# A hybrid encoder layer: convolution turned by halves of its channels, projections dealt out anew, and sums of the up projection in PSUM

## The chip, the cores and the metric

The kernel runs on one core of a Trainium2 chip. The metric is the device time of one execution in microseconds (us); a comparison takes the median of several runs. PE is TensorE, DVE is VectorE, ACT is ScalarE, POOL is GpSimd, SP is SyncE, which here only issues DMAs.

## The reference

One layer works on x (2048 tokens x 1024), in float32.

```python
proj = x @ w_in                       # 1024 -> 3*512 (Hyena) + 3*512 (attention) + 512 (memory queries)
y_h = hyena_mixer(hy_u, ...)          # short convolution, then twice: z = x_i * fft_long_conv(z)
y_d = diff_attention(rope(dq), rope(dk), dv, ...)   # 4 heads, two halves of 64
y_m = memory_attention(mq, mem, w_kv)               # 256 memory tokens
x = layer_norm(ALPHA * x + concat(y_h, y_d, y_m) @ w_out)
h = dwconv3(x @ w_up) ; g, u = split(h)             # 2 x 2816 columns
x = layer_norm(ALPHA * x + (silu(g) * u) @ w_down)
```

`fft_long_conv` multiplies the spectrum of the input, zero-padded to 4096 points, with that of a filter, which a small network makes from the positions.

## The kernel before

Matrix products of full precision are made of three passes: each operand is split into a high part and a low part, and `mm3` (line 146) adds high x high, high x low and low x high in PSUM. The split of a weight chunk is an ACT cast and a subtraction on POOL or DVE (`low`, line 144).

The kernel runs as five stages in a row: `project` (line 679), `diff_attention`, `out_proj`, `ffn_up` (line 1214) and `ffn_down`.

`project` has two weaves (`weave`, line 661). Each has a main generator and a fill generator. Every yield of the main work earns a credit of 6144 x R x its weight (1.0 if it names none), and the fill is stepped until the credit is used up, in columns that pass through PE. In the first weave `spectra` makes the filter spectra and the fill is the Hyena projections (`proj_u`); R is R1. In the second `conv` makes the two long convolutions and the fill is the memory projections, the queries, keys and values (`proj_qk` with the rotary embedding, `proj_v`), and the memory attention; R is R2. What is left of the fill when the main work ends runs alone. A scheduler then orders the instructions of each engine by a simulation of its own, so the order on an engine follows that of issue only roughly; `keep_in_program_order` pins single instructions. `after(cols, f)` (line 539) issues f when that many more columns have been issued to PE.

The FFT of 2048 points as 128 x 16 works on S, a tile of [128, 32, 256]: 32 rows of 256 channels. There are four runs (two orders x two halves of the 512 channels). In each, `first` multiplies 8 loads of [128, 2 rows, 256 channels] with the matrices `st` (lines 248, 249); the four DVE transposes of `turn` (line 253, 64 channels each) turn S in 32x32 blocks; `middle` takes 16 pairs of rows through a block product (line 273), the product with the filter's spectrum on DVE (lines 393 to 400), and a second block product back into S (line 405); `turn` again; `last` multiplies with `sb` (line 419), gates with the loaded `hu` on DVE (line 421) and stores to `zd` or `yh`. `middle` needs all channels of its rows, so all four transposes; `first` and `last` of one row need only their own channels. `pipeline` (line 232) staggers the steps of such a part. The `last` of a run and the `first` of the next share one pipeline.

`hu` (the three Hyena inputs after their short convolution) is written to DRAM by `turn_u` (line 570) in the first weave.

`ffn_up` multiplies by Winograd's form of Strassen's scheme: a unit (128 columns of gate and up over 1024 tokens) is seven products, each of 12 matmuls of 512 columns, b11, t2, t1, t3, b21, b22, t4, with operands made beforehand (`weight`, line 1239: DVE and POOL make the sums `s`, ACT and POOL split them, up to nine products ahead). Each product has a PSUM tile of its own out of six, and its result is combined with the partial sums p1, u2, u3, u4 on DVE (line 1290) into the two rows that the width-3 convolution reads (ACT line 1317, DVE scalar_tensor_tensor line 1319). There are 44 units, 22 for each half of the tokens.

Of the kernel before, what the change touches and what calls it, by code (L numbers as in the profile page):

```python
# [10 lines left out]
F32 = mybir.dt.float32  # L11
# [10 lines left out]
HW = 512  # L22
# [107 lines left out]
class Trunk:  # L130
# [15 lines left out]
    def mm3(self, out, sh, sl, mh, ml, start, stop):  # L146

        mm = self.nc.tensor.matmul
        mm(out, sh, mh, start=start, stop=False)  # L149
        mm(out, sh, ml, start=False, stop=False)  # L150
        mm(out, sl, mh, start=False, stop=stop)  # L151
# [99 lines left out]
    NT, WTB, WTT, WTC = 4, 1.0, 0.8, 1.95  # L251

    def turn(self, S):

        for c in range(0, CH, 64):
            v = S[:, :, c:c + 64].rearrange("p t c -> p c t")
            t = self.nc.vector.transpose(v, v)
            if c == 128:
# [82 lines left out]
    def load_u(self, t, i, u, hs):  # L341
        for k in range(2):
            self.dma(t[:, k], self.hu[i][:, 2 * u + k, :, hs])

# [8 lines left out]
    def conv(self, yp, sp, ph):  # L353
# [5 lines left out]

        def first(o, h):  # L360
            hs = slice(CH * h, CH * h + CH)

            def a0(u):
                xa[u] = self.hy(sp, "kr")
                if o:
                    self.dma(xa[u], self.zd[h][:, 2 * u:2 * u + 2])
                else:
                    self.load_u(xa[u], 0, u, hs)

            def a1(u):  # L370
                p = xa.pop(u)
                self.stage1(S, ph, u, p, p)

            return a0, a1
# [34 lines left out]
        def last(o, h):  # L409
            hs = slice(CH * h, CH * h + CH)  # L410

            def c0(u):
                xb[u] = self.hy(sp, "kr")
                self.load_u(xb[u], 1 + o, u, hs)

            def c1(u):
                ps = self.hy(ph, "h")
                for par in range(2):
                    nc.tensor.matmul(ps, self.sb[:, par], S[:, 16 * par + 2 * u:16 * par + 2 * u + 2], start=(par == 0), stop=(par == 1))
                z = self.hy(sp, "t")  # L420
                nc.vector.tensor_tensor(z, ps, xb.pop(u), ALU.mult)
                dst = self.zd[h] if o == 0 else self.yh.rearrange("(t1 t2) c -> t1 t2 c", t2=16)[:, :, hs]
                self.dma(dst[:, 2 * u:2 * u + 2], z)

            return c0, c1
# [4 lines left out]
        def both(*fs):  # L430
            def f(u):
                for g in fs:
                    g(u)
            return f

        yield from self.pipeline(8, first(*runs[0]))
        for i, run in enumerate(runs):
            yield from self.turn(S)
            yield from self.pipeline(16, middle(*run), self.WTB)
            yield from self.turn(S)  # L440
            c0, c1 = last(*run)
            if i + 1 < len(runs):
                a0, a1 = first(*runs[i + 1])
                yield from self.pipeline(8, [c0, a0, c1, a1], self.WTC)
            else:
                yield from self.pipeline(8, [c0, skip, c1])
# [100 lines left out]
    def proj_u(self, st, pp, quarter, ahead):  # L547
        nc = self.nc
        for cc in range(12):
# [11 lines left out]
            nat = lambda v: v.rearrange("p (t1 t2) -> p t1 t2", t2=16)  # L561
            nc.vector.tensor_scalar(t, h[:, 1:513], cw[:, 1, cc:cc + 1], self.cb[:, cc:cc + 1], ALU.mult, ALU.add)
            nc.vector.scalar_tensor_tensor(t, h[:, 0:512], cw[:, 0, cc:cc + 1], t, ALU.mult, ALU.add)
            nc.vector.scalar_tensor_tensor(tp.rearrange("p b (r t1) -> p t1 (b r)", r=4), nat(h[:, 2:514]),
# [3 lines left out]
    LATE = 17000  # L568

    def turn_u(self, st, pt, quarter, cc, tp):  # L570
# [6 lines left out]
        dst = self.hu[cc // 4][quarter].rearrange("(b r) t1 c -> (r t1) b c", r=4)  # L577
        nc.scalar.dma_start(dst[:, :, 128 * (cc % 4):128 * (cc % 4) + 128], ev)

    def proj_qk(self, pp, t0, rope, cc):  # L580
# [14 lines left out]
        nc.vector.tensor_tensor(q, q, rope[:, 0], ALU.mult)  # L595
        nc.gpsimd.tensor_tensor(rot, rot, rope[:, 1], ALU.mult)
        nc.vector.tensor_tensor(q, q, rot, ALU.add)
        out = self.s2.tile([128, 2, 512], F32R, name="qo", tag="hl", bufs=self.HL)
        nc.scalar.copy(out[:, 0], q)
        self.low(nc.vector, out[:, 1], q, out[:, 0])  # L600
        self.dma(self.qk[cc // 4][cc % 4][:, :, t0:t0 + 512], out)
# [72 lines left out]
    NB1, WIDE, HL = {}, 4, 2  # L674
    NB2 = dict(c_m2=4, c_ma=6, kr=6, ki=4, t=4)
    R1 = 0.605
    R2 = 0.521
# [536 lines left out]
    def ffn_up(self):  # L1214
# [5 lines left out]
        with ExitStack() as ctx:  # L1220
# [51 lines left out]
            def product(n, ps, name):  # L1272
                wh, wl = ops.pop(n)
                xh, xl = self.xo[name]
                for k in range(4):
                    self.mm3(ps, wh[:, k], wl[:, k], xh[:, k], xl[:, k], k == 0, k == 3)
                    next(fill, None)

            def unit(u):
                s, c = divmod(u, NF)  # L1280
                rows = [hp.tile([128, 1027], F32, name=f"row{g}", tag=f"row{g}") for g in range(2)]
                for g in range(2):
                    if s == 0:
                        nc.gpsimd.memset(rows[g][:, 1:2], 0.0)
                    else:
# [3 lines left out]
                p1, u2, u3, u4 = (sp.tile([128, 512], F32, name=t, tag="u", bufs=5) for t in ("p1", "u2", "u3", "u4"))  # L1289
# [8 lines left out]
                for j, (name, f) in enumerate(steps):  # L1298
                    weight(7 * u + j + self.AHEAD)
                    ps = pp.tile([128, 512], F32, name="pu", tag="u")  # L1300
                    product(7 * u + j, ps, name)
                    f(ps)
                    if j == 2:
                        p5 = ps
                    elif j == 3:
                        add(out[1][1], p5, u3)
                    elif j == 5 and stores:
# [201 lines left out]
```

## Time and profile before

| what | us |
|---|---|
| median of 3 runs | 3761.63 (3761.15 to 3763.39) |
| the profiled execution | 3758.56 |
| its span, first to last instruction | 3756.8 |
| PE busy | 3503.8 (93%) |
| DVE busy | 2548.0 (68%) |
| ACT busy | 1537.9 (41%) |
| POOL busy | 1711.6 (46%) |

The mean granted clock of TensorE is 0.965 of full speed. Matmuls overlap, so the duration of one (0.39 us) is more than the distance from one to the next. Times in the rows are counted from the first instruction. A row of waits names who waited, for whom, the total in us, how often, and the longest. A row of windows gives the stretch, its length, the busy time of each engine with the number of instructions in brackets, the granted clock, the busy share of the DMA engines and GB/s. A row of the timeline gives start, duration, engine, line, operation, tiles and shapes, the count of merged instructions, and in brackets the idle time before and what ended it.

### The profile page before, as it was taken

The numbers are of one execution on the slowest core, as the hardware profiler recorded it, in microseconds if no ns is written. First come the engines' busy times: TensorE is split into PE (matmuls) and PEld (weight loads), VectorE is DVE, ScalarE is ACT, GpSimd is POOL, SyncE is SP. The second block draws the span as 40 slices with busy tenths as digits, with TensorE's granted clock in tenths as the row PEclk, the third lists the DMA queues.
The fourth block names the chain that finished last, engine by engine and source line by source line (L and its number), as shares of the span: only waits on it lengthen the run. The fifth ranks groups of instructions, "written<-read, shape, count | busy, mean of one in ns | idle before, by whom it ended". The sixth has DMA issues, their size and how long they took to land.

```text
span 3756.8 us, 48083 instructions
## 1 busy us (share of the span) xinstructions
PE 3503.8 (93%) x16952; PEld 2843.6 (76%) x16952; DVE 2548.0 (68%) x2952; ACT 1537.9 (41%) x2903; POOL 1711.6 (46%) x1484
## 2 busy tenths in 40 slices
PE   8899988888888879999999998999989999899998
PEld 7788877565757667877877886887767888688887
DVE  7667647575857649888985444777877888622565
ACT  4443443333323337787884101433344443421211
POOL 3222313222222336666664223888866888610333
PEclk9999999999999989999999998999999999999999
DMA  6655568576757571213213445322233223443553
GB/s 161 194 176 164 181 194 216 168 209 191 205 170 193 155 170 44 75 41 86 58 42 104 138 151 174 87 79 83 75 116 96 80 82 84 168 141 113 175 180 132
DMA packets 536069, 502.43 MB, mean 134 GB/s; under 512 B 78216, under 2 KB 416780, under 8 KB 534292
## 3 DMA queue, kind: packets, MB, share of 16 engines
q1 hardware_dynamic: 273236, 343.08, 31.0%
q10 hardware_dynamic: 262592, 156.27, 14.4%
q8 instruction: 135, 2.21, 0.2%
q14 instruction: 106, 0.87, 0.1%
HBM read 369.20 MB, written 121.63 MB: 131 GB/s over the span
## 4 chain that ended last, share of the span: by engine, by line
PE 49%; POOL 5%; DMA 3%; DVE 2%; ACT 2%; issue 1%; ACTq 0%; SPq 0%; POOLq 0%; DVEq 0%
PE ps L149 7%; PE ps L151 7%; PE ps L150 7%; PE pu L149 5%; PE pu L150 5%; PE pu L151 5%; PE po L860 5%; POOL al L144 3%; PE pt L852 3%; PE ps L820 2%; PE ps L821 2%; DMA xr<-in_w_out_dram 1%; DVE t L1319 1%; POOL t L1322 1%; ACT t L1317 1%
## 5 line engine op out<-in xcount | busy, mean ns | idle before, releaser
L144 POOL TENSOR_TENSOR wl<-wr,wh 128x512 fp32r<-128x512 f32 x180 | 243.4, 1354 | 699.6 <-ACT wh L504 421.1
L149 PE MATMUL pu<-slot,ah 128*128 128x512 f32 x1232 | 491.2, 399 | 9.5 <-ACT slot L1056 5.6
L150 PE MATMUL pu<-slot,ah 128*128 128x512 f32 x1232 | 488.1, 396 | 0.0
L151 PE MATMUL pu<-slot,al 128*128 128x512 f32 x1232 | 486.4, 395 | 0.0
L149 PE MATMUL pp<-xh,wh 128*128 128x512 f32 (+2 forms) x1344 | 475.1, 354 | 10.0 <-ACT wh L504 3.7
L151 PE MATMUL pp<-xh,wl 128*128 128x512 f32 (+2 forms) x1344 | 457.3, 341 | 5.2 <-POOL wl L144 3.8
L150 PE MATMUL pp<-xl,wh 128*128 128x512 f32 (+2 forms) x1344 | 454.2, 338 | 0.9 <-DVE xl L144 0.9
L823 DVE TENSOR_REDUCE st<-ps 128x1 f32<-128x1024 f32 x256 | 312.1, 1220 | 55.1 <-PE ps L821 53.7
L1319 DVE SCALAR_TENSOR_TENSOR t<-row,fcw,t 128x1023 f32<-128x1023 f32 (+1 forms) x176 | 286.3, 1646 | 91.5 <-ACT t L1317 90.0
L144 POOL TENSOR_TENSOR al<-s,ah 128x512 fp32r<-128x512 f32 x176 | 294.7, 1676 | 35.5 <-ACT ah L1266 29.8
L827 ACT ACTIVATE e<-ps,st 128x1024 f32<-128x1024 f32 x256 | 287.1, 1124 | 35.1 <-DVE st L823 33.1
L149 PEld LDWEIGHTS pp<-xh,wh 128*128 128x128 f32 x1344 | 258.5, 192 | 48.5 <-issue 18.4
L151 PEld LDWEIGHTS pp<-xh,wl 128*128 128x128 f32 x1344 | 258.2, 192 | 41.9 <-issue 12.5
L150 PEld LDWEIGHTS pp<-xl,wh 128*128 128x128 f32 x1344 | 259.1, 193 | 35.4 <-issue 14.2
L149 PEld LDWEIGHTS pu<-slot,ah 128*128 128x128 f32 x1232 | 232.7, 189 | 69.9 <-DVE u L1290 8.5
L820 PE MATMUL ps<-kk,q 128*128 128x512 f32 x512 | 253.7, 495 | 26.2 <-DMA kk<-qk 15.1
L151 PEld LDWEIGHTS pu<-slot,al 128*128 128x128 f32 x1232 | 232.5, 189 | 55.5
L150 PEld LDWEIGHTS pu<-slot,ah 128*128 128x128 f32 x1232 | 233.4, 189 | 53.3
L151 PE MATMUL ps<-slot,gl 128*128 128x512 f32 x689 | 270.9, 393 | 0.0
L150 PE MATMUL ps<-slot,gh 128*128 128x512 f32 x689 | 270.7, 394 | 0.0
L149 PE MATMUL ps<-slot,gh 128*128 128x512 f32 x689 | 270.6, 393 | 0.0
L860 PE MATMUL po<-at,v 128*128 128x256 f32 x1024 | 269.3, 387 | 0.8
(228 smaller groups left out, 7869.6 us busy)
## 6 DMA issues: line engine op xcount, KB each, us to landing
wr<-in_w_in_dram ACTq DMA_DIRECT2D x224, 256.0 KB
slot<-in_ffn_w_up_dram ACTq DMA_DIRECT2D x88, 512.0 KB
gr<-gd SPq DMA_DIRECT2D x63, 448.0 KB
gd<-t SPq DMA_DIRECT2D x66, 256.0 KB
xr<-in_x_dram SPq DMA_DIRECT2D x64, 256.0 KB
dec<-in_c_dec_dram SPq DMA_DIRECT2D x32, 512.0 KB
c_m<-in_c_m_dram SPq DMA_DIRECT2D x128, 128.0 KB
kd<-ev ACTq DMA_DIRECT2D x64, 256.0 KB
```

The lines of the kernel that those rows point to most:

```text
L144: eng.tensor_tensor(lo, src, hi.bitcast(F32), ALU.subtract)
L149: mm(out, sh, mh, start=start, stop=False)
L150: mm(out, sh, ml, start=False, stop=False)
L151: mm(out, sl, mh, start=False, stop=stop)
L820: self.tc.keep_in_program_order(nc.tensor.matmul(o, qh, kk[c][:, ks], start=True, stop=False))
L821: self.tc.keep_in_program_order(nc.tensor.matmul(o, ql, kk[c][:, ks], start=False, stop=True))
L823: nc.vector.tensor_reduce(m, ps, AX.X, ALU.max, negate=True)
L827: nc.scalar.activation(e[:, 1024 * t:1024 * t + 1024], ps, AF.Exp, bias=m, accum_out=col(6 + 2 * t))
L852: self.tc.keep_in_program_order(nc.tensor.transpose(ps[:, j], e[:, 512 * g + 128 * j:512 * g + 128 * j + 128], self.ident))
L860: self.tc.keep_in_program_order(nc.tensor.matmul(P["ps"], P["v"][:, kb], P["at"][kb // 4][:, kb % 4], start=(kb == 0), stop=(kb == 15)))
L1317: nc.scalar.activation(v, rows[g][:, c0:c1], AF.Identity, bias=cb[:, cc:cc + 1], scale=cw[:, 1, cc:cc + 1])
L1319: nc.vector.scalar_tensor_tensor(v, rows[g][:, c0 + k - 1:c1 + k - 1], cw[:, k, cc:cc + 1], v, ALU.mult, ALU.add)
```

## The change

- `S` is worked in the outer stages by halves of its channels: `first` and `last` take [128, 4 rows, 128 channels] at a time, the four steps of one half before those of the other. Two of the four transposes (`turn_half`) remain at each boundary; the other two are issued inside the outer pipelines (`turns`).
- DRAM tiles `hu` and `zd` are laid out by quarters of the channels, and `turn_u` writes in that layout.
- The weights of the yields and the ratios R1 and R2 are new, so the fill is dealt out otherwise.
- The rotary arithmetic is issued 6500 columns after the projection, its split and store after 10500. Its tiles have 8 buffers in place of 4.
- In `ffn_up` a unit has three PSUM tiles, pa, pb and pc. b11 and then b21 are added in pa, t2, t3 and t4 in pb, t1 and b22 in pc; between them DVE or ACT reads the sums so far. `u4` is gone, and the first row's first half is an ACT copy.

```diff
-    def mm3(self, out, sh, sl, mh, ml, start, stop):
+    def mm3(self, out, sh, sl, mh, ml, start, stop, more=False):
...
-        self.hu = [t(f"hu{k}", [4, 16, 32, HW]) for k in range(3)]
-        self.zd = [t(f"zd{h}", [128, 16, CH]) for h in range(2)]
+        self.hu = [[t(f"hu{k}{p}", [128, 16, 128]) for p in range(4)] for k in range(3)]
+        self.zd = [t(f"zd{p}", [128, 16, 128]) for p in range(4)]
...
-    NT, WTB, WTT, WTC = 4, 1.0, 0.8, 1.95
+    NT, WTT, WTB, WTC, WTH = 4, 1.63, 0.92, 1.08, 1.0
+
+    def turn_part(self, S, i):
+
+        v = S[:, :, 64 * i:64 * i + 64].rearrange("p t c -> p c t")
+        return self.nc.vector.transpose(v, v)
...
+    def turn_half(self, S, p):
+        for i in range(2):
+            t = self.turn_part(S, 2 * p + i)
+            if i == 0:
+                self.tc.keep_in_program_order(t)
+            yield self.WTH
+        for _ in range(2):
+            yield self.WTH
...
+        def rows(par, v):
+
+            p, u = v // 4, v % 4
+            return S[:, 16 * par + 4 * u:16 * par + 4 * u + 4, 128 * p:128 * p + 128]
+
         def first(o, h):
...
+            def a0(v):
+                p, r = part(v)
+                xa[v] = quarter(self.hy(sp, "kr"))
+                self.dma(xa[v], (self.zd if o else self.hu[0])[2 * h + p][:, r])
+
+            def a1(v):
+                x = xa.pop(v)
+                for par in range(2):
+                    ps = quarter(self.hy(ph, "h"))
+                    nc.tensor.matmul(ps, self.st[:, par], x, start=True, stop=True)
+                    nc.scalar.copy(rows(par, v), ps)
...
-        yield from self.pipeline(8, first(*runs[0]))
+        def turns(plan):
+
+            def f(v):
+                for i in plan.get(v, ()):
+                    self.tc.keep_in_program_order(self.turn_part(S, i))
+            return f
+
+        a0, a1 = first(*runs[0])
+        yield from self.pipeline(8, [a0, skip, skip, a1, turns({3: (0,), 5: (1,)})], self.WTC)
         for i, run in enumerate(runs):
-            yield from self.turn(S)
+            yield from self.turn_half(S, 1)
             yield from self.pipeline(16, middle(*run), self.WTB)
-            yield from self.turn(S)
+            yield from self.turn_half(S, 0)
             c0, c1 = last(*run)
+            c0 = both(turns({0: (2,), 2: (3,)}), c0)
             if i + 1 < len(runs):
                 a0, a1 = first(*runs[i + 1])
-                yield from self.pipeline(8, [c0, a0, c1, a1], self.WTC)
+                yield from self.pipeline(8, [c0, a0, c1, a1, turns({3: (0,), 5: (1,)})], self.WTC)
             else:
-                yield from self.pipeline(8, [c0, skip, c1])
+                yield from self.pipeline(8, [c0, skip, c1], self.WTC)
...
     LATE = 17000
+    ROT = (6500, 10500)
...
+        def turned():
+            nc.vector.tensor_tensor(q, q, rope[:, 0], ALU.mult)
+            nc.gpsimd.tensor_tensor(rot, rot, rope[:, 1], ALU.mult)
+            nc.vector.tensor_tensor(q, q, rot, ALU.add)
...
+        self.after(self.ROT[0], turned)
+        self.after(self.ROT[1], parted)
...
-    NB1, WIDE, HL = {}, 4, 2
+    NB1, WIDE, HL = {}, 8, 2
...
-    R1 = 0.605
-    R2 = 0.521
+    R1 = 0.52
+    R2 = 0.81
...
-                steps = (("b11", lambda p: nc.scalar.copy(p1, p)),
-                         ("t2", lambda p: add(u2, p, p1)),
-                         ("t1", lambda p: add(u4, p, u2)),
-                         ("t3", lambda p: add(u3, p, u2)),
-                         ("b21", lambda p: add(out[0][0], p, p1)),
-                         ("b22", lambda p: add(out[0][1], p, u4)),
-                         ("t4", lambda p: add(out[1][0], p, u3)))
+                pa, pb, pc = (pp.tile([128, 512], F32, name=t, tag="u") for t in ("pa", "pb", "pc"))
+
+                def after_t3():
+                    add(u3, pb, p1)
+                    add(out[1][1], pc, u3)
+
+                steps = (("b11", pa, lambda: nc.scalar.copy(p1, pa)),
+                         ("t2", pb, lambda: add(u2, pb, p1)),
+                         ("t1", pc, None),
+                         ("t3", pb, after_t3),
+                         ("b21", pa, lambda: nc.scalar.copy(out[0][0], pa)),
+                         ("b22", pc, lambda: add(out[0][1], pc, u2)),
+                         ("t4", pb, lambda: add(out[1][0], pb, p1)))
```

`last` changes as `first` does: one load of `hu` per step, and `rows(par, v)` as the moving operand. `quarter` views a tile of [128, 2, 256] as [128, 4, 128], and `part(v)` gives the half and the four rows of step v.

## Rows read from the trace of the kernel before

**Rows 1.** Windows of stages: length, PE, PEld, DVE, ACT, POOL busy, clock, DMA.

```profile
0.00:527.00 527.00, 484.92 (x3296) 434.11 (x3297) 360.01 (x376) 220.12 (x429) 149.86 (x113) 0.95 0.59 178
...
527.00:1290.00 763.00, 650.74 (x2806) 490.09 (x2805) 498.03 (x617) 256.17 (x548) 191.85 (x167) 0.93 0.67 189
1290.00:1373.00 83.00, 80.99 (x406) 66.83 (x405) 31.94 (x52) 37.09 (x84) 40.17 (x34) 1.00 0.62 164
...
2342.00:3246.00 904.00, 884.42 (x3816) 710.81 (x3815) 728.32 (x642) 362.27 (x523) 719.53 (x574) 0.99 0.30 86
```

**Rows 2.** Waits of PE, first row of 0 to 527, the others of 527 to 1290.

```profile
PE h L273 <- DVE S L257: 25.7, 4, 9.1
...
PE h L419 <- DVE S L257: 33.8, 4, 11.2
PE h L273 <- DVE S L257: 20.2, 3, 10.9
...
PE h L248 <- DMA kr<-hu: 4.4, 4, 1.8
```

**Rows 3.** Windows of turns plus 12 us: the first stage's four, the convolution's eight.

```profile
sum 116.60, PE 90.41 PEld 84.61 DVE 101.78 ACT 36.23 POOL 21.61; mean PE 22.60 PEld 21.15 DVE 25.45 ACT 9.06 POOL 5.40
...
573.70:603.50 29.80, 19.84 (x95) 16.25 (x96) 29.24 (x29) 9.60 (x23) 7.71 (x6) 0.84 0.91 216
...
1246.80:1275.80 29.00, 21.94 (x74) 13.51 (x73) 23.86 (x19) 6.41 (x17) 6.17 (x8) 0.82 0.39 120
sum 232.50, PE 162.94 PEld 116.32 DVE 203.97 ACT 63.77 POOL 55.47; mean PE 20.37 PEld 14.54 DVE 25.50 ACT 7.97 POOL 6.93
```

**Rows 4.** Timeline of one turn of the convolution, 690 to 760.

```profile
697.24 17.08 DVE L257 STREAM_TRANSPOSE S<-S 128x2048 f32<-128x2048 f32 x4
...
707.03 0.39 PE L151 MATMUL pp<-xh,wl 128*128 128x512 f32 x1
...
714.38 3.78 PE L419 MATMUL h<-S,sb 128*128 128x512 f32 x4 [6.96 <-DVE S L257]
```

**Rows 5.** Windows between turns, sums: four middle stretches, then four outer ones.

```profile
sum 353.00, PE 327.82 PEld 273.36 DVE 246.77 ACT 131.09 POOL 104.39; mean PE 81.95 PEld 68.34 DVE 61.69 ACT 32.77 POOL 26.10
...
sum 130.80, PE 121.87 PEld 72.68 DVE 39.46 ACT 43.00 POOL 24.35; mean PE 30.47 PEld 18.17 DVE 9.86 ACT 10.75 POOL 6.09
```

**Rows 6.** Waits of DVE in the convolution, 527 to 1290.

```profile
DVE q L595 <- DMA rot<-q: 65.0, 15, 9.2
```

**Rows 7.** Windows of the up projection: ten units, ten units, twenty units.

```profile
2832.00:3222.00 390.00, 390.00 (x1681) 315.61 (x1680) 331.26 (x276) 155.30 (x219) 317.98 (x256) 1.00 0.27 75
2364.00:2559.00 195.00, 195.00 (x842) 157.85 (x840) 155.52 (x136) 77.99 (x110) 161.53 (x127) 1.00 0.28 79
2559.00:2760.00 201.00, 197.77 (x841) 156.91 (x839) 158.25 (x140) 76.39 (x110) 165.07 (x131) 1.00 0.28 79
```

**Rows 8.** Timeline of one unit of the up projection: PE, DVE and ACT.

```profile
2605.30 0.40 PE L151 MATMUL pu<-slot,al 128*128 128x512 f32 x1
...
2609.95 5.16 DVE L1319 SCALAR_TENSOR_TENSOR t<-row,fcw,t 128x1023 f32<-128x1023 f32 x3
2615.03 0.68 DVE L1290 TENSOR_TENSOR u<-pu,p 128x512 f32<-128x512 f32 x1
2616.29 2.88 DVE L1250 TENSOR_TENSOR s<-slot 128x512 f32<-128x512 f32 x1 [0.59 <-POOL s L1250]
...
2620.36 1.76 DVE L1250 TENSOR_TENSOR s<-s,slot 128x512 f32<-128x512 f32 x1 [0.58 <-POOL al L144]
...
2622.76 0.69 DVE L1290 TENSOR_TENSOR row<-pu,u 128x512 f32<-128x512 f32 x1
...
2627.00 1.24 ACT L1317 ACTIVATE t<-row,fcb,fcw 128x1023 f32<-128x1023 f32 x1
...
2628.28 1.28 DVE L1319 SCALAR_TENSOR_TENSOR t<-row,fcw,t 128x1023 f32<-128x1023 f32 x1 [3.03 <-ACT t L1317]
```

**Rows 9.** Waits of PE from the end of the up projection on, 3246 to 3757.

```profile
PE ps L149 <- DVE row L1290: 13.8, 1, 13.8
```

More of the change, by code (lines that the diff above doesn't have):

```diff
@@ L144, in low @@
         eng.tensor_tensor(lo, src, hi.bitcast(F32), ALU.subtract)
-    def mm3(self, out, sh, sl, mh, ml, start, stop):
+    def mm3(self, out, sh, sl, mh, ml, start, stop, more=False):
         mm = self.nc.tensor.matmul
-        mm(out, sh, mh, start=start, stop=False)
-        mm(out, sh, ml, start=False, stop=False)
-        mm(out, sl, mh, start=False, stop=stop)
+        mm(out, sh, mh, start=start, stop=False, skip_group_check=more)
+        mm(out, sh, ml, start=False, stop=False, skip_group_check=more)
+        mm(out, sl, mh, start=False, stop=stop, skip_group_check=more)
     def scratch(self, ctx):
@@ L249, in stage1 @@
             nc.scalar.copy(S[:, 16 * par + 2 * u:16 * par + 2 * u + 2], ps)
-    NT, WTB, WTT, WTC = 4, 1.0, 0.8, 1.95
+    NT, WTT, WTB, WTC, WTH = 4, 1.63, 0.92, 1.08, 1.0
+    def turn_part(self, S, i):
+        v = S[:, :, 64 * i:64 * i + 64].rearrange("p t c -> p c t")
+        return self.nc.vector.transpose(v, v)
     def turn(self, S):
[L255 to L258, printed above, removed]
+        for i in range(4):
+            t = self.turn_part(S, i)
+            if i == 2:
                 self.tc.keep_in_program_order(t)
@@ L339, in filters @@
                 yield from self.pipeline(16, [g0, skip, g1])
-    def load_u(self, t, i, u, hs):
-        for k in range(2):
-            self.dma(t[:, k], self.hu[i][:, 2 * u + k, :, hs])
     ENG = ["pppv"]
@@ L409, in last, with c0, c1 @@
         def last(o, h):
[L410 to L417, printed above, removed]
-                for par in range(2):
[L419 to L423, printed above, removed]
+            def c0(v):
+                p, r = part(v)
+                xb[v] = quarter(self.hy(sp, "kr"))
+                self.dma(xb[v], self.hu[1 + o][2 * h + p][:, r])
+            def c1(v):
+                p, r = part(v)
+                ps = quarter(self.hy(ph, "h"))
+                for par in range(2):
+                    nc.tensor.matmul(ps, self.sb[:, par], rows(par, v), start=(par == 0), stop=(par == 1))
+                z = quarter(self.hy(sp, "t"))
+                nc.vector.tensor_tensor(z, ps, xb.pop(v), ALU.mult)
+                q = 2 * h + p
+                dst = self.zd[q] if o == 0 else self.yh.rearrange("(t1 t2) c -> t1 t2 c", t2=16)[:, :, 128 * q:128 * q + 128]
+                self.dma(dst[:, r], z)
             return c0, c1
@@ L594, in proj_qk, with parted @@
             self.dma(rot[32 * b:32 * b + 32], q[s:s + 32])
[L595 to L601, printed above, removed]
+        def turned():
+            nc.vector.tensor_tensor(q, q, rope[:, 0], ALU.mult)
+            nc.gpsimd.tensor_tensor(rot, rot, rope[:, 1], ALU.mult)
+            nc.vector.tensor_tensor(q, q, rot, ALU.add)
+        def parted():
+            out = self.s2.tile([128, 2, 512], F32R, name="qo", tag="hl", bufs=self.HL)
+            nc.scalar.copy(out[:, 0], q)
+            self.low(nc.vector, out[:, 1], q, out[:, 0])
+            self.dma(self.qk[cc // 4][cc % 4][:, :, t0:t0 + 512], out)
+        self.after(self.ROT[0], turned)
+        self.after(self.ROT[1], parted)
         yield
@@ L1270, in weight, with product @@
                     self.up_raw(u + 2)
-            def product(n, ps, name):
+            def product(n, ps, name, first):
                 wh, wl = ops.pop(n)
@@ L1275, in product @@
                 for k in range(4):
-                    self.mm3(ps, wh[:, k], wl[:, k], xh[:, k], xl[:, k], k == 0, k == 3)
+                    self.mm3(ps, wh[:, k], wl[:, k], xh[:, k], xl[:, k], first and k == 0, k == 3, not first)
                     next(fill, None)
@@ L1288, in unit @@
                 out = [[rows[g][:, 2 + 512 * t:514 + 512 * t] for t in range(2)] for g in range(2)]
[L1289 removed]
+                p1, u2, u3 = (sp.tile([128, 512], F32, name=t, tag="u", bufs=5) for t in ("p1", "u2", "u3"))
                 add = lambda o, x, y: nc.vector.tensor_tensor(o, x, y, ALU.add)
[L1291 to L1307 removed]
+                pa, pb, pc = (pp.tile([128, 512], F32, name=t, tag="u") for t in ("pa", "pb", "pc"))
[9 more added lines that the diff above has]
+                         ("t4", pb, lambda: add(out[1][0], pb, p1)))
+                for j, (name, ps, f) in enumerate(steps):
+                    weight(7 * u + j + self.AHEAD)
+                    product(7 * u + j, ps, name, j < 3)
+                    if f:
+                        f()
+                    if j == 5 and stores:
                         store(*stores.pop())
```

24 lines of the change are left out of this document (8 added, 16 removed).

## The prediction

> **What bounds the kernel now.** I read the stages' windows first, then who waited for whom in each. TensorE (PE) is busy in every stage and ends the kernel, so time can come only from its idle stretches, from its slower clock, or from new waits put into its order. [rows 1] gives the idle time. The first stage (filter spectra as main work, the Hyena projections woven in as fill) is 527 us long with 42 idle. The convolution, up to its last output at 1290, is 763 us with 112 idle at a mean clock of 0.93. The 83 us after it hold projections alone, with 2 idle. The up projection is 904 us with 20 idle. Since the last two are nearly full, the convolution is the place to look, and [rows 2] names its cause: PE waits for the DVE transposes of S, 54 us directly in the convolution and 26 in the first stage. Everything else in that list is small (the loads of `hu` cost 4.4 us).
>
> [rows 3] widens the view to each turn (four transposes) plus 12 us, since the clock falls after an idle spell. In the convolution eight such stretches lose 232.5 - 162.9 = 69.6 us of PE. Their granted clock is 0.84 in the first and 0.82 in the last, so 9.5 to 10.4 us of each 29 run at the lower of the two levels, where a matmul takes twice as long. If all idle time (8.7 us a turn) lies inside, the clock costs under 1 us a turn; if none does, 5. I take 2.6, so 21 for eight: a turn's price is 91 us in all. The first stage's four turns lose 116.6 - 90.4 = 26.2 us idle, and 8 more for the clock in the same proportion: 34 us.
>
> [rows 4] shows one turn. DVE holds 17.1 us of transposes; PE works on projections for 9.8 us after their start, runs out of them, and stands 7 us until S is turned.
>
> **The unit of fill.** One unit is 6144 columns, 12 matmuls of 512. In [rows 7] ten units of `ffn_up`, 84 such matmuls each, take 195.0 us, so one is 0.232 us and a fill unit 2.79. A yield of the main work earns weight x R units.
>
> **Change 1, the first stage.** A turn there earned 8 x 0.8 x 0.605 = 3.9 units, 10.8 us against 17 of transposes. It now earns 8 x 1.63 x 0.52 = 6.8 units, 18.9 us: the transposes are covered. The other 33 yields of a run earn 33 x (0.605 - 0.52) = 2.8 units, 7.8 us, less. This was taken from stretches that are nearly full (42 - 26 = 16 us idle in the rest of the stage, its start included), with main work still there to do. The total stays the same (162 yields' worth at 0.605, 188 at 0.52: 98 units each), so no fill is left over. Bounds: -34 if nothing else opens, -12 if thinner fill exposes other waits. I take **-28**.
>
> **Change 2, half turns.** Before, a turn in the convolution earned 8 x 0.8 x 0.521 = 3.3 units, 9.3 us, against 17.1. Now two of the four transposes stand at a boundary (8.5 us) with 4 x 1.0 x 0.81 = 3.2 units, 9.0 us, beside them. The other two are issued inside the outer pipelines, after the steps that fill their half of the channels and before the steps that read it. Nothing is removed: 32 transposes, the same matmuls, the same columns. Sixteen transposes only move to where DVE has room: in the four outer stretches of [rows 5] it is busy 39.5 of 130.8 us. There a transpose of 4.3 us can stand ahead of the product `z` (line 421), which frees a PSUM tile that PE needs two steps later. Bound: nothing, to 16 x 4.3 = 69 us if PE always waited it out. A step holds some 3 us of convolution and as much fill, so I stay near nothing: I leave 20 of the 91 us, for all of this together.
>
> **Change 3, projections spread.** By the weights the convolution earned 121 units and now earns 151, against some 155 wanted in all. The tail of pure projections goes into the stage. This gains nothing by itself, as the tail was full; it is the cover that change 2 uses. If the cover ran out before the convolution did, its last pipeline would stand bare.
>
> **Change 4, rotary later.** `q*rope` overwrites what the DMA `rot<-q` still reads, so it stands at the head of DVE's queue until that lands: 65.0 us in 15 waits [rows 6]. Behind it stand the products of `middle`, the turns and the weights' low parts. POOL's `rot*rope` waits likewise, with the low parts `wl` behind it. Issued 6500 columns (3 us of fill, more with convolution between) later, most of it is gone. The four rotary DMAs keep their place on SP's queue; the store of `qo` moves some 10500 columns back, so loads queued behind it on SP are held up less. PE's own idle time in the four middles is 353.0 - 327.8 = 25 us [rows 5]; I credit 9 of it. Changes 2 to 4 come to 91 - 20 + 9 = **-80**; bounds -115 (turns and most of the middle's idle gone) and -40.
>
> **Costed at nothing.** Loads of `hu` fall from two to one per step, with longer pieces; `yh` is stored in shorter ones. They are issued two or three steps ahead behind the fill, and uncovered would cost about the 4.4 us of [rows 2]. `out_proj`, the attention and `ffn_down` keep their code.
>
> **Change 5, sums in PSUM.** It removes two DVE additions (`u4`, and `out00`, which becomes an ACT copy) per unit of 44. PE isn't relieved: the number of matmuls stays. But each unit now has three PSUM tiles instead of seven, and PE may not add t3 into `pb` before DVE has read t2 from it, nor b22 into `pc` before DVE has read t1. [rows 8] shows how late DVE is. In that unit t2's last matmul begins at 2605.30, and `u2` only at 2615.03, ending at 2615.71; t3 would be due after t1's 2.8 us, at 2608.3. Today that lateness is harmless until the six tiles run out: units take 19.5 us at first and 20.1 once they have [rows 7].
>
> The new loop from the same rows: `u2` begins, DVE waits for POOL before `s1` and again before `s2`, then `u3` and `out11`, which ends at 2623.45, 8.4 us after `u2` began. Then PE may start b22 (2.8), DVE adds `out01` (0.9 with the hand-over), ACT scales the row (1.3), and the first STT of the convolution begins; from it (one period before 2628.28, at 2608.14) to `u2` are 6.9 us. Together 20.3 to 20.4 us, 0.9 over PE's 19.5. Removing `u4` doesn't help, for `s2` waits for POOL anyway. So 42 x 0.9 = 38, less the 6 us that PE loses today in ten units, less some 8 of the 13.8 us wait at the end [rows 9], since DVE can no longer be far behind: 24, of which I take **+20**. Bounds: -14 (`u3` comes ahead of `s2`, the loop is open; 6 + 8 come back) and +45.
>
> "PSUM — Partial Sum Buffer" of the Trainium skill (section "PSUM bank collisions raise a hardware error") has it that a bank must be guarded as a whole: no engine may read one while a matmul writes any part of it. By that rule every added group waits for its reader in full; were DVE as late as in [rows 8], that is 7.4 us in each of 43 units, and the sum would be some 320 us worse. No run here shows it yet; the rows' own loop, which lets PE's wait bring DVE closer, gives the 20 above.
>
> **Sum.** -28 - 80 + 20 = -88. The profiled execution took 3758.56 us (span 3756.8), 3.1 under the runs' median of 3761.63, so the median should become 3674.
>
> **Rivals.** (A, forecast, 0.50) as above, 3674; its own range 3650 to 3700. (B, 0.22) the loop in `ffn_up` is open: -28 - 80 - 14, 3640. For it: the order on DVE is the scheduler's and may change; against it: `s1` and `s2` stand ahead of `u3` in these rows, and nothing in the diff moves them. (C, 0.14) the turns are covered by half only, since the fill's own DVE work (the weights' low parts, the sums of the memory attention) delays the transposes: -14 - 40 + 20, 3728. For it: the measured waits exceed 17.1 - 9.3. (D, 0.08) slower: one more item before `u3` in DVE's order, as both weight sums with their waits (3.5 us) between t2's end and `u2`, makes the loop 23.9 us: 42 x 4.4 = 185, so -28 - 80 + 185 - 14 = +63, 3825. It decides from 108/43 = 2.5 us a unit, a unit of 22.0. (E, 0.03) the turns' waits come back elsewhere and all is within 0.2%, which is about what a measurement tells from no change; with parts of C's and D's neighbours, 0.04. The rest, 0.03, lies between A and C.
>
> **Range.** 3615 to 3730: A, B and C but for their edges. Faster 0.88, same 0.04, slower 0.08.
>
> **What would show it.** PE's waits for S in the two stages under 15 us in all; the clock there 0.97 or more; the attention beginning some 105 us earlier. `q*rope` waiting a third as long. In `ffn_up` a unit of 20 to 20.6 us, with PE waiting for DVE before b22. I am wrong if PE still waits for S by more than 40 us, or a unit takes over 21 us or stays at 19.5.

## The result, and the profile after

The changed kernel takes 3653.47 us, the median of 4 runs (3652.62 to 3657.72), beside 3762.26 of the kernel before on the same chip: a ratio of 0.971, 95% interval 0.970 to 0.973. It is 109 us faster where 88 were predicted; the time lies inside the range, 20 us under the forecast. The profiled execution took 3654.12 us (span 3652.2), 104.4 less than that of before.

The sum came out better than its terms. Here are the stretches of both traces, cut at the same events: the convolution's first matmul, the last matmul of the projections, and the first and last of `ffn_up` and `ffn_down`. (In after the last product that `ffn_up` works on is b22, in `pc`.)

| stretch | before, us | after, us | difference | predicted |
|---|---|---|---|---|
| first stage | 530.6 | 526.4 | -4.2 | -28 |
| convolution with the projections left over | 841.6 | 755.0 | -86.6 | -80 |
| attention and `out_proj` | 969.2 | 969.1 | 0 | 0 |
| `ffn_up` | 900.3 | 901.2 | +0.9 | +28 |
| from its last matmul to `ffn_down`'s first | 13.8 | 0.9 | -12.9 | -8 |
| `ffn_down` | 490.3 | 488.7 | -1.6 | 0 |

The windows of after over the first two stretches (as in [rows 1]):

```profile
0.00:526.40 526.40, 488.59 (x3348) 440.73 (x3349) 362.10 (x382) 223.34 (x436) 152.46 (x115) 0.96 0.58 182
526.40:1281.40 755.00, 699.69 (x3155) 537.78 (x3154) 530.33 (x663) 287.99 (x624) 229.73 (x200) 0.98 0.73 206
```

and the one of before that answers to the second of them, with its tail of pure projections:

```profile
530.60:1372.20 841.60, 727.49 (x3186) 552.97 (x3185) 527.84 (x665) 291.19 (x627) 232.02 (x201) 0.94 0.66 187
```

PE's idle time there falls from 114.1 us (841.60 - 727.49) to 55.3. Its busy time falls by another 27.8 at a granted clock of 0.98 instead of 0.94. The work is not quite the same: counted in both traces, 30 matmuls of fill, 7168 columns, have moved from this stretch into the first stage. At the 0.232 us that a matmul of 512 columns takes in [rows 7] that is some 3.3 us. For equal work the first stage gains some 7.5 us and the convolution some 83, of which about 24 are clock.

PE's waits of after in the first stage, then in the convolution (as in [rows 2]):

```profile
PE pp L151 <- DVE wl L144: 11.5, 4, 4.3
PE h L285 <- DVE S L256: 8.7, 1, 8.7
...
PE pt L600 <- DVE tp L589: 3.2, 2, 2.1
```

```profile
PE h L434 <- DVE S L256: 16.8, 4, 5.9
...
PE pt L958 <- POOL me L950: 3.6, 2, 3.2
```

In the convolution the waits for S fell from 54.0 us to 16.8, and nothing large took their place. DVE's timeline over one outer stretch shows the transposes one at a time, with its other work between them:

```profile
728.15 4.29 DVE L256 STREAM_TRANSPOSE S<-S 128x2048 f32<-128x2048 f32 x1 [1.07 <-ACT S L387]
...
743.96 4.26 DVE L256 STREAM_TRANSPOSE S<-S 128x2048 f32<-128x2048 f32 x1
748.09 0.67 DVE L436 TENSOR_TENSOR t<-h,kr 128x512 f32<-128x512 f32 x1
...
753.29 4.30 DVE L256 STREAM_TRANSPOSE S<-S 128x2048 f32<-128x2048 f32 x1 [1.08 <-ACT S L387]
...
766.19 4.54 DVE L256 STREAM_TRANSPOSE S<-S 128x2048 f32<-128x2048 f32 x1
```

In the first stage they fell from 25.7 to 8.7, but a line that [rows 2] lacked now leads: 11.5 us for `wl`, the low part of a projection weight. There are four turns. In the first PE still waits 8.7 us for S; in the other three it waits 3.6, 4.3 and 3.3 for `wl`. The timeline of DVE and of PE in one of these shows why.

```profile
209.48 13.00 DVE L256 STREAM_TRANSPOSE S<-S 128x2048 f32<-128x2048 f32 x3 [0.64 <-ACT S L249]
222.29 0.74 DVE L144 TENSOR_TENSOR wl<-wr,wh 128x512 fp32r<-128x512 f32 x1
...
225.29 4.43 DVE L256 STREAM_TRANSPOSE S<-S 128x2048 f32<-128x2048 f32 x1
```

```profile
219.16 0.29 PE L150 MATMUL pp<-xl,wh 128*128 128x256 f32 x1
223.08 0.39 PE L151 MATMUL pp<-xh,wl 128*128 128x258 f32 x1 [3.64 <-DVE wl L144]
```

Here there is fill enough, but the fill itself needs DVE: every fourth low part is made there, and this one stood behind three transposes. PE waited 3.64 us for it.

Windows of the up projection (as in [rows 7]) over ten units and over nineteen, and PE's waits in it for other engines' results:

```profile
2271.40:2469.00 197.60, 196.80 (x842) 157.42 (x841) 151.19 (x121) 88.16 (x123) 159.47 (x131) 1.00 0.28 78
2749.50:3124.00 374.50, 372.41 (x1595) 298.41 (x1594) 279.87 (x230) 163.34 (x233) 321.21 (x250) 1.00 0.28 76
```

```profile
PE pb L149 <- DVE u L1323: 4.8, 4, 4.4
...
PE pc L149 <- DVE row L1323: 2.7, 8, 1.3
...
PE ps L149 <- ACT slot L1399: 0.9, 1, 0.9
```

A unit takes 19.8 us, later 19.7, and PE waits for a reader of its PSUM tiles by 7.5 us in all 44 units. The predicted loop isn't there. The wait of 13.8 us at the end [rows 9] is 0.9, and that is the whole gain: the stage itself is as long as before. DVE's order is another:

```profile
2473.37 0.69 DVE L1323 TENSOR_TENSOR row<-pb,p 128x512 f32<-128x512 f32 x1 [0.69 <-PE pb L151]
2474.12 1.28 DVE L1354 SCALAR_TENSOR_TENSOR t<-row,fcw,t 128x1023 f32<-128x1023 f32 x1
2475.32 0.68 DVE L1323 TENSOR_TENSOR u<-pb,p 128x512 f32<-128x512 f32 x1
2475.92 3.95 DVE L1354 SCALAR_TENSOR_TENSOR t<-row,fcw,t 128x1023 f32<-128x1023 f32 x2
```

`u2`, the reader that PE needs, now stands behind one STT (`SCALAR_TENSOR_TENSOR`) of the unit before; in the unit after this one it stands ahead of all four (2490.28), and ahead of the additions that read that unit's b22 and t4 (2492.48 and 2494.56), so PE takes up t2 of the next unit before it is through with this one. In [rows 8] `u2` came after all four STTs.

### The profile page after: what moved, and what is told of

Its sections match the earlier page's. It is cut to its first block, busy times and chain, and to the rows that moved or that the text cites. A ratio compares the mean times of both kernels' runs of the same rounds, so it can differ in the third digit from the quotient of the medians.

```text
span 3652.2 us, 47939 instructions
## 1 busy us (share of the span) xinstructions
PE 3473.1 (95%) x16952; PEld 2827.6 (77%) x16952; DVE 2473.0 (68%) x2864; ACT 1568.3 (43%) x2947; POOL 1707.1 (47%) x1484
## 4 chain that ended last, share of the span: by engine, by line
PE 59%; DVE 10%; DMA 6%; issue 3%; POOL 2%; ACT 2%; SPq 1%; ACTq 0%; POOLq 0%; DVEq 0%
PE ps L151 7%; PE ps L149 7%; PE ps L150 7%; PE po L893 5%; DVE t L1354 3%; PE pt L885 3%; PE ps L853 3%; PE ps L854 3%; PE pb L149 2%; PE pb L151 2%; PE pb L150 2%; DVE s L1283 2%; PE pc L149 2%; PE pc L150 2%; PE pc L151 2%
## 5 line engine op out<-in xcount | busy, mean ns | idle before, releaser
L1354 DVE SCALAR_TENSOR_TENSOR t<-row,fcw,t 128x1023 f32<-128x1023 f32 (+1 forms) x176 | 319.3, 1835 | 8.9 <-ACT t L1352 7.2
L144 POOL TENSOR_TENSOR al<-s,ah 128x512 fp32r<-128x512 f32 x176 | 280.5, 1598 | 88.3 <-ACT ah L1299 75.5
L150 PEld LDWEIGHTS pp<-xl,wh 128*128 128x128 f32 x1344 | 260.0, 193 | 35.6 <-issue 15.1
L1399 ACT CAST gh<-gr 128x896 fp32r<-128x896 f32 (+1 forms) x94 | 91.9, 978 | 343.2 <-PE ps L150 336.8
L529 ACT CAST wh<-wr 128x512 fp32r<-128x512 f32 x240 | 149.2, 623 | 189.7 <-PE pp L150 113.3
L875 POOL TENSOR_SCALAR e<-e,st 128x1024 f32<-128x1024 f32 x64 | 128.6, 2009 | 203.7 <-PE ps L854 167.2
L144 DVE TENSOR_TENSOR gl<-gr,gh 128x896 fp32r<-128x896 f32 (+1 forms) x94 | 130.5, 1389 | 136.1 <-ACT gh L1399 135.5
L256 DVE STREAM_TRANSPOSE S<-S 128x2048 f32<-128x2048 f32 x48 | 208.6, 4393 | 15.3 <-ACT S L387 7.4
L149 PE MATMUL pb<-slot,ah 128*128 128x512 f32 x528 | 208.5, 399 | 5.1 <-DVE u L1323 4.8
```

Of the source, the lines that this page charges most:

```text
L144: eng.tensor_tensor(lo, src, hi.bitcast(F32), ALU.subtract)
L149: mm(out, sh, mh, start=start, stop=False, skip_group_check=more)
L150: mm(out, sh, ml, start=False, stop=False, skip_group_check=more)
L256: return self.nc.vector.transpose(v, v)
L529: self.nc.scalar.copy(hi, r)
L875: nc.gpsimd.tensor_scalar(es[1][:, lo], es[1][:, lo], st[:, 14:15], 1.0, ALU.mult, ALU.mult)
```

## The experiments

Ratios are to the kernel before on the same chip, with a 95% interval. "After" is the changed kernel, 0.9713 (0.9696 to 0.9730); differences in us are differences of the ratios times 3762, and carry some 8 us of uncertainty.

**The first stage's credit undone.** In after:

```diff
-    NT, WTT, WTB, WTC, WTH = 4, 1.63, 0.92, 1.08, 1.0
+    NT, WTT, WTB, WTC, WTH = 4, 0.8, 0.92, 1.08, 1.0
-    R1 = 0.52
+    R1 = 0.605
```

> The changed kernel with the first stage's weight of a turn (0.8) and ratio (0.605) as before; all else as changed (3653 us). Theory N, from the two traces: the first stage gained only some 8 us, because the fill in a turn now waits for the low parts of its weights, which DVE makes behind the transposes; so this runs 5 to 10 us longer than the changed kernel, 3658 to 3664. Theory P, the prediction's step: the turns were covered, so this runs 28 us longer, 3681.

Measured: 3665.09 us, 0.9735 (0.9722 to 0.9748), 8 us slower than after. The waits for S are back at 25.8 us. So change 1 is worth 4 us (by the table) to 8 (by this run, and by the table for equal work), not 28.

**Low parts of the first stage on POOL alone.**

```diff
-            self.ws = self.stream_w(wp, cols, lambda i: self.eng(0))
+            self.ws = self.stream_w(wp, cols, lambda i: nc.gpsimd if i < 96 else self.eng(0))
```

> The changed kernel, but in the first stage all low parts of the weights are made on POOL (before: every fourth on DVE). Theory N: PE's four waits for DVE's wl (11.5 us) and the slower clock after them go, 10 to 16 us less than the changed kernel, 3638 to 3644, and PE's waits for S in that stage stay under 12 us. Rival: POOL's subtraction takes 1.37 us against 0.79, POOL becomes late in place of DVE, and the time stays within 5 us of 3653.

Measured: 3660.16 us, 0.9724 (0.9709 to 0.9738), 4 us slower than after, which can't be told from none. My theory fell. Of the waits in the first stage, `wl` on DVE is gone, and the next operation in the same queue has its place (S still 7.7):

```profile
PE pt L600 <- DVE tp L589: 15.4, 5, 5.1
PE h L285 <- DVE S L256: 7.7, 1, 7.7
```

`tp` is the short convolution's output, also made on DVE behind the transposes. Which product PE waits for changes; that the transposes hold DVE doesn't.

**The transposes of the first stage apart**, with the rotary at once (below), which makes no difference clear of the noise. Each is pinned, two yields of fill behind it:

```diff
-            if i == 2:
-                self.tc.keep_in_program_order(t)
+            self.tc.keep_in_program_order(t)
+            yield self.WTT
             yield self.WTT
-        for _ in range(self.NT):
-            yield self.WTT
```

> The changed kernel with the rotary arithmetic at once and, in the first stage's turns, each transpose issued on its own with two yields of fill behind it and all four pinned in program order, so that the fill's own DVE work can stand between them. Theory (the first stage keeps its idle time because the low parts and the S wait behind three transposes in a row): the waits for low parts and S fall from 20 us to under 10, and the kernel takes 3640 to 3646. Rival (another wait takes their place, as with the low parts on POOL): within 4 us of the run with the rotary at once, 3647 to 3655.

Measured: 3652.6 us, 0.9711 (0.9694 to 0.9727): the rival. The transposes do stand apart, at 212.55, 220.27, 227.10 and 236.22 in the turn shown above. S is ready later by that much:

```profile
PE h L283 <- DVE S L256: 12.3, 3, 8.7
...
PE pp L151 <- DVE wl L144: 6.8, 4, 2.4
PE pt L598 <- DVE tp L587: 5.5, 3, 2.4
```

The three add up to 24.6 us, against 23.4 in after. Three ways of ordering DVE in these turns give the same idle time in other names.

**The rotary at once**, in after: `turned()` and `parted()` are called where they were put off.

> The changed kernel, but the rotary arithmetic, its split and its store are issued right after the loads of rot, as before. The prediction's step: 9 us more than the changed kernel (0 to 20), 3653 to 3673, and DVE's wait of q*rope for rot back from 30 to about 65 us. Rival: DVE's freedom from that wait is what keeps the turns covered, over 25 us more, above 3678.

Measured: 3651.12 us, 0.9696 (0.9677 to 0.9716), 6 us faster than after and within the uncertainty. DVE's longest wait is what it was in after (29.5 in 15) and not what it was before (65.0 in 15 [rows 6]):

```profile
DVE q L623 <- DMA rot<-q: 30.6, 15, 4.5
```

So the later issue neither shortens this wait nor gains time. What halved it, the eight buffers or the new spread, wasn't tried.

**The spread alone**, the kernel before with R2 raised so that the convolution earns nearly all projections:

```diff
-    R2 = 0.521
+    R2 = 0.655
```

> The kernel before with R2 at 0.655 in place of 0.521 and nothing else, so that the projections last to the end of the convolution with whole turns. The prediction's arithmetic: a turn earns 4.2 units, 11.7 us, against 9.3; 2.4 us a turn and some clock, 20 to 35 us less than before, 3727 to 3742. Rival (the spread carries the gain): 60 us or more less than before, under 3702.

Measured: 3764.58 us, 1.0004 (0.9989 to 1.0019): nothing. The tail is gone (the last output of the convolution comes at 1367.5 instead of 1281.8), and the waits for S stand:

```profile
PE h L419 <- DVE S L257: 35.2, 4, 13.1
PE h L273 <- DVE S L257: 17.8, 2, 14.8
```

More credit per turn (4.2 units for 3.3) didn't cover more of it.

**All four transposes at the boundary**, in after, with half channels in the outer steps kept:

```diff
-        for i in range(2):
-            t = self.turn_part(S, 2 * p + i)
-            if i == 0:
+        for i in range(2):
+            for k in range(2):
+                t = self.turn_part(S, 2 * i + k)
+                if i == k == 0:
...
-            c0 = both(turns({0: (2,), 2: (3,)}), c0)
-                yield from self.pipeline(8, [c0, a0, c1, a1, turns({3: (0,), 5: (1,)})], self.WTC)
+                yield from self.pipeline(8, [c0, a0, c1, a1, skip], self.WTC)
```

> The changed kernel, but all four transposes stand at the boundary again, with the same credit of fill beside them; channels by halves, loads, weights of the yields, spread of the fill and the late rotary work stay. If the half turns carry the gain of the convolution: 8 waits of about 8 us come back and some clock with them, 55 to 80 us more than the changed kernel, 3708 to 3733. Rival: the spread of the fill and the later rotary work carry it, under 20 us more, below 3673.

Measured: 3666.42 us, 0.9744 (0.9729 to 0.9760), 12 us slower than after. The expected 55 and more did not come, but the edit hadn't made whole turns: since an outer step still touches one half of the channels only, transposes could start ahead of the boundary (at 735.37, then 758.86, then 777.76 in one turn), and `last` could start after two (transposes in a row from 691.95, `last` from 700.55 in another). That turn's four transposes stand in a row as in before, and yet PE waits for S by 15.1 us in the whole convolution, no more than in after. So the start on a half seems to weigh more than the gaps between transposes; no run parts the two. The next run takes the halves themselves away.

**Full channels again.** In after, `first`, `last`, `load_u`, `turn_u`, `hu` and `zd` of before, four transposes at a boundary with the same 3.2 units:

```diff
-            ps = quarter(self.hy(ph, "h"))
+            ps = self.hy(ph, "h")
...
-                    nc.tensor.matmul(ps, self.sb[:, par], rows(par, v), start=(par == 0), stop=(par == 1))
+                    nc.tensor.matmul(ps, self.sb[:, par], S[:, 16 * par + 2 * u:16 * par + 2 * u + 2], start=(par == 0), stop=(par == 1))
...
-        for i in range(2):
-            t = self.turn_part(S, 2 * p + i)
-            if i == 0:
+        for i in range(4):
+            t = self.turn_part(S, i)
+            if i == 2:
                 self.tc.keep_in_program_order(t)
             yield self.WTH
-        for _ in range(2):
-            yield self.WTH
```

> The changed kernel, but first and last work again on [128, 2 rows, 256 channels] with the old layout of hu and zd, and all four transposes stand at each boundary with the same credit of fill beside them (3.2 units); the spread of the projections, the later rotary and the up projection stay. Theory (the channel halves carry the convolution's gain, because two transposes lie under outer steps that need only the other half): TensorE's waits for S in the convolution come back to some 55 us from 17, and the clock with them; 50 to 75 us slower than the changed kernel, 3703 to 3728. Rival (the spread and the credit carry it): under 25 us slower, waits for S under 30.

Measured: 3759.6 us, 1.0000 (0.9988 to 1.0012), 108 us slower than after: on the theory's side, beyond its upper end. The convolution's window and PE's waits in it:

```profile
529.90:1395.30 865.40, 724.53 (x3151) 552.20 (x3152) 527.82 (x663) 288.91 (x624) 228.63 (x199) 0.91 0.64 180
```

```profile
PE h L437 <- DVE S L256: 34.1, 3, 14.2
PE pt L959 <- POOL me L951: 21.9, 4, 8.6
PE pt L499 <- DVE xl L144: 19.6, 2, 12.7
PE h L283 <- DVE S L256: 11.4, 1, 11.4
```

Idle time is 140.9 us, 85.6 more than in after, and the clock costs 24.8 of busy time. Only 45.5 us are waits for S. Of the rest 19.6 are fill that waits for `xl`, the low part of the tokens, and 21.9 fill that waits for POOL (`me`). The stretch is also 24 us longer than in before (841.6), so the 108 us are what the halves are worth under the new deal of the fill, and not against before. Two turns, first one in which PE waits for S and then one in which it waits for `xl`:

```profile
932.76 16.34 DVE L256 STREAM_TRANSPOSE S<-S 128x2048 f32<-128x2048 f32 x4
...
934.59 0.39 PE L151 MATMUL pp<-xh,wl 128*128 128x512 f32 x1
...
949.15 3.78 PE L437 MATMUL h<-S,sb 128*128 128x512 f32 x4 [14.18 <-DVE S L256]
```

```profile
584.38 12.21 DVE L256 STREAM_TRANSPOSE S<-S 128x2048 f32<-128x2048 f32 x3 [3.79 <-ACT S L249]
...
596.49 1.33 DVE L144 TENSOR_TENSOR xl<-pt,xh 128x512 fp32r<-128x512 f32 x2
```

```profile
597.27 1.11 PE L499 MATMUL pt<-ident,xr 128*128 128x128 f32 x4 [12.70 <-DVE xl L144]
```

In the first PE works for 2 us and then stands 14; next in its order is `last`, which needs S. In the second the fill is next in its order, but it waits 12.7 us for an `xl` that DVE makes right after the transposes. There the cover exists, but it is locked behind the thing that it should cover.

**Full channels with full cover.** As that, with eight yields in a turn, so that it earns 6.2 units, 17 us, and less elsewhere (WTB 0.72, WTC 0.87, WTH 0.95).

> As the run on full channels, but each turn earns 6.2 units of fill (17 us) against its four transposes; the weights of the other yields are lowered so that the same total is dealt out. Theory (halves are needed, for the fill that a boundary earns is drawn out of it): TensorE still waits for S by 40 us or more, within 15 us of the run on full channels. Rival (enough cover does the same as the halves, as the prediction's sum of cover against transposes has it): waits for S under 25 us, within 15 us of the changed kernel's 3653.

Measured: 3743.5 us, 0.9955 (0.9939 to 0.9972); 16 us under the run before, just outside the 15 that the theory gave, and 91 above after, where the rival had 15. The stretch of the convolution takes 847.1 us. PE waits for S by 55.6 us, and for low parts as in that run:

```profile
PE h L438 <- DVE S L256: 43.7, 4, 14.2
PE pt L500 <- DVE xl L144: 20.4, 2, 12.2
PE h L284 <- DVE S L256: 11.9, 2, 10.7
```

Doubling the cover does not replace the halves.

**The up projection.** First after with the sums of before, then before with the new sums.

> The changed kernel with the up projection as before (a PSUM tile for each product, seven additions). Theory N: the stage itself is as long either way (901 us in both traces), and only the 13.8 us wait at its end comes back: 12 to 16 us more than the changed kernel, 3666 to 3669. Theory P, the prediction's step: sums in PSUM cost 20, so this is 20 us faster, 3633.

Measured: 3675.27 us, 0.9766 (0.9752 to 0.9780), 20 us slower than after; `ffn_up` takes 903.0 us, and 13.2 pass before `ffn_down`, which are the wait of [rows 9]. DVE's order is that of [rows 8] again: three STTs at 2605.49, then `u2` at 2610.56.

> The kernel before with the up projection's sums in PSUM and nothing else. Theory N: the wait at the stage's end goes and the stage is as long as before, 10 to 18 us less than before, 3744 to 3752. Theory P, the prediction's step: 20 us more than before, 3782.

Measured: 3748.21 us, 0.9952 (0.9936 to 0.9968), 18 us faster than before; `ffn_up` takes 899.2 us, and 1.1 pass before `ffn_down`. So both directions give -18 to -20 (14 by the two stretches of these traces), where the prediction has +20. DVE's order is like that of after, with `u2` ahead of three STTs in the unit shown and ahead of all four in the next (2634.22):

```profile
2619.34 1.60 DVE L1321 SCALAR_TENSOR_TENSOR t<-row,fcw,t 128x1023 f32<-128x1023 f32 x1 [0.85 <-ACT t L1319]
2620.87 0.68 DVE L1290 TENSOR_TENSOR u<-pb,p 128x512 f32<-128x512 f32 x1
2621.47 4.09 DVE L1321 SCALAR_TENSOR_TENSOR t<-row,fcw,t 128x1023 f32<-128x1023 f32 x2
```

So the new order comes with the new sums and goes with them.

**u2 pinned** behind the instruction issued before it (`keep_in_program_order` around its addition).

> The changed kernel, but the addition u2 is pinned behind everything issued before it on DVE, so behind the four convolution instructions of the unit before, which is the order that the prediction assumed. If that order makes the loop of 20.3 us: the mean unit goes from 19.7 to 20.3 or more, 20 to 30 us more than the changed kernel, 3673 to 3684, with PE waiting for DVE before t3 or b22. Rival: the loop was overrated whatever the order, under 5 us more, below 3659.

Measured: 3662.84 us, 0.9727 (0.9709 to 0.9745), 5 us slower than after, between the two expectations. The pin names `s3` of the same unit, not the STTs, and DVE's order stayed nearly what it was. This run tells nothing of the order.

**The order pinned.** `s3`, `u2` and the four STTs pinned, which puts both `s3` and `u2` behind the four STTs of the unit before:

```diff
-("t2", pb, lambda: add(u2, pb, p1)),
+("t2", pb, lambda: self.tc.keep_in_program_order(add(u2, pb, p1))),
-                    src = add(3, nc.vector, a11, a21, ALU.subtract)
+                    src = add(3, nc.vector, a11, a21, ALU.subtract, True)
...
-                        nc.vector.scalar_tensor_tensor(v, rows[g][:, c0 + k - 1:c1 + k - 1], cw[:, k, cc:cc + 1], v, ALU.mult, ALU.add)
+                        self.tc.keep_in_program_order(nc.vector.scalar_tensor_tensor(v, rows[g][:, c0 + k - 1:c1 + k - 1], cw[:, k, cc:cc + 1], v, ALU.mult, ALU.add))
```

(the `True` pins `s3` likewise)

> The changed kernel with DVE's order in the up projection pinned to the one that the prediction assumed: the four STTs of the unit before, s3, u2, s1, s2, u3, out11. Theory (the predicted loop is real, and was open only because the order put u2 ahead of two STTs in every other unit): a unit takes 20.2 to 20.6 us instead of 19.75, the up projection is 19 to 36 us longer, TensorE waits for DVE before b22; 3672 to 3690. Rival (the loop was mis-sized, whatever the order): unit under 19.9 us, within 6 us of 3653.

Measured: 3932.89 us, 1.0450 (1.0430 to 1.0471): 277 us slower than after, far outside what either theory gave. `ffn_up` takes 1175.1 us; ten units take 261.4 us, 26.1 each. PE's waits there, then DVE, ACT and PE in one unit:

```profile
PE pb L149 <- ACT ah L1301: 126.8, 41, 8.2
```

```profile
3085.70 6.20 DVE L1356 SCALAR_TENSOR_TENSOR t<-row,fcw,t 128x1025 f32<-128x1025 f32 x4 [1.38 <-ACT t L1354]
3091.82 0.68 DVE L1283 TENSOR_TENSOR s<-slot 128x512 f32<-128x512 f32 x1
3092.42 0.68 DVE L1325 TENSOR_TENSOR u<-pb,p 128x512 f32<-128x512 f32 x1
```

```profile
3092.53 0.62 ACT L1301 CAST ah<-s 128x512 fp32r<-128x512 f32 x1 [3.13 <-DVE s L1283]
```

```profile
3090.17 0.39 PE L151 MATMUL pc<-slot,al 128*128 128x512 f32 x1
3093.24 0.47 PE L149 MATMUL pb<-slot,ah 128*128 128x512 f32 x1 [2.68 <-ACT ah L1301]
```

t3 needs the cast of `s3` (done at 3093.15) and a `pb` that `u2` has read (done at 3093.10). Both stand behind the four STTs, and the two releases lie 0.05 us apart. So an order on DVE can close a loop. But it is not the order that the prediction assumed. In the trace of before `s3` of the next unit stands ahead of the STTs, which in [rows 8] begin at 2628.28:

```profile
2623.37 0.68 DVE L1250 TENSOR_TENSOR s<-slot 128x512 f32<-128x512 f32 x1
```

Here it stands behind them, and it is the cast of `s3` that PE waits for by name. Whether the guard on `pb` would close a loop without `s3` stays open: a run with `u2` alone behind the STTs wasn't made. Nor does the run say what before's sums would cost in this order.

## Why the prediction was right, and where it wasn't

- **Changes 2 to 4, -80: right in size (-86.6), with the wrong reason for its parts.** The step "it is the cover that change 2 uses" counted cover in microseconds of fill. With full cover and no halves the stretch of the convolution is no shorter than in before (847.1 us against 841.6; 3743.5 in all, with the gain of the new sums in it), and the spread without halves gains nothing (3764.58); taking the halves out of after loses all of 108 us. What works is that half of the transposes come one at a time, with 5 to 12 us between them in the stretch shown, together with that an outer step needs only its half. Which of the two does more isn't shown; the run with all four at the boundary speaks for the second. That the spread adds to the halves wasn't tried by itself: no run has halves with the old spread. The 9 us credited to the later rotary are not there.
- **Change 1, -28: mis-sized, it measured 4 to 8.** The step "the transposes are covered" failed. In the first turn PE still waits 8.7 us for S. In the other three it failed not by the amount of fill, but because the fill's `wl` and `tp` wait in DVE's queue behind the same transposes. Even its cautious bound, -12, was too good, and case C had named the mechanism ("the fill's own DVE work"), for a part of the time.
- **Change 5, +20: wrong sign, it measured -12 by the table, -18 to -20 by the two exchanges.** The step that failed is the last leg of the loop: the 6.9 us from the first STT of a unit to `u2`, taken from [rows 8], where `u2` stands behind all four STTs. `s1` and `s2` did stay ahead of `u3`, as "nothing in the diff moves them" has it; but `u2` moved ahead of three of the STTs or of all four. The diff moves nothing by hand, yet the new sums alone bring that order and the old ones take it back. The lower bound, -14, was this case (B), at 0.22. That the order is what opened the loop is argued from the traces; the pinned run doesn't test it, for it holds back `s3` too, and so its 277 us are no price of the predicted loop. The rule of "PSUM — Partial Sum Buffer" of the Trainium skill (section "PSUM bank collisions raise a hardware error"), that a bank is guarded as a whole, makes every added group wait for its reader; the trace of after has 7.5 us of that in all units, because most readers come early.
- **What it looked for.** Waits for S: 25.5 us in the two stages, over the 15 looked for and under the 40 that would refute it. Clock: 0.96 and 0.98, where 0.97 or more was looked for in both. The attention begins at 1295.9, 91 us earlier, not 105. The wait of `q*rope` halved, where a third was looked for, and for another reason than its later issue. A unit of `ffn_up` takes 19.7 to 19.8 us, neither the 20 and more of the loop nor 19.5; PE's waits before b22 are 2.7 us in all.

Two terms missed by 20 to 24 and by some 32 to 40 us in opposite directions, so that the total was off by only 20. That it fits is luck, and no evidence for its terms.

## What to carry to other kernels

Count cover by what it needs, not by its length: here fill hid an engine's long operation only as far as it didn't itself wait in that engine's queue. Breaking the long operation up so that the queue could serve others between the pieces, and the next stage could start on a half, gained here what the fill tried did not. Standing apart alone gained nothing in the first stage, whose next step needs the whole. When a change adds readers that an engine waits for, look first at where they stand in their engine's order, and take the order from the new trace, not from the old one.

## What the runs showed of the hardware beyond that

In two pairs of runs idle time came with a lower clock. For the same number of matmuls in the convolution, within five on record, PE was busy 699.7 us at a granted clock of 0.98 in after and 724.5 at 0.91 on full channels: 24.8 us on top of 85.6 of idle time. In the up projection with the pinned order the clock fell to 0.89 from 1.00, and ten units kept PE busy for 226.5 us instead of 196.8, with 841 and 842 matmuls on record. A DVE transpose of 128x2048 in float32 took 4.26 to 4.54 us in the rows of after above, and three or four in a row kept DVE's other work waiting for 12.2 to 17.1.
